# First norm of a decoder trunk: squares of two token chunks summed with tokens on the partitions, channel factors put into x

## The chip, the cores and the metric

The kernel runs on one core of a Trainium2 chip. The metric is the device time of one execution in microseconds. The engines are PE (matmul), PEld (its weight loads), DVE (VectorE), ACT (ScalarE), POOL (GpSimd) and SP (the queue that issues most DMAs).

## The reference, cut to what matters

A trunk of two layers works on 1040 tokens (16 meta tokens and 1024 inputs) of 1024 channels: a Conformer convolution layer, then a differential-attention layer, then a last norm. Only the start of the first layer matters here:

```
def rms_norm(x, gain):
    y = x * lax.rsqrt(jnp.mean(x * x, axis=-1, keepdims=True) + EPS)
    return y * gain

proj = jnp.einsum("bld,dc->blc", rms_norm(h, norm_gain[0]), w_in)
u, g, z = jnp.split(proj, 3, axis=-1)          # 2048 channels each
v = u * jax.nn.sigmoid(g)
v = depthwise convolution over 31 tokens of v  # then a layer norm, silu, times silu(z), a projection
```

So each token has one scale, the inverse root of the mean of its squared channels, and each channel one factor, `norm_gain`.

## The kernel before, in words

Everything is kept with channels on the partitions: `x_t[k]` (k = 0 to 7) holds 128 channels by 1040 tokens in float32, the tokens ordered even ones first, then odd ones. A projection is made as three passes of matmuls with operands split in a high part (rounded to the matmul's float32r) and a low part (the rest): high by high, high by low, low by high (`passes`, L202 to L209). A weight strip is 1024 channels by 128 outputs: it is loaded into `wf` (L174), copied to `wh` by ACT (L190), and `wl` is the difference (L191, written by the helper `lo_part`, L158). `wh` and `wl` have two buffers each, and so has `wf`. The tokens are taken in three chunks of 348, 346 and 346 (`CH`, L34).

The start of the kernel (L330 to L416) has parts that are called in the order of the string `ORDER` (L70), each for one chunk:

- `unscaled` (u, L379): ACT copies x to the high part (L384), DVE or POOL makes the low part (L386, the string `LOU` says which engine).
- `statistics` (t, L353): the eight tiles are squared, all on ACT for chunks 1 and 2, on ACT and DVE in turn for chunk 0 (L362, L365). Eight matmuls with a matrix of ones (L368, plain float32) sum the squares over all channels and spread the sum over the 128 partitions. `rstd_from` (L211) makes the inverse root on 128 x 346 elements: logarithm, exponential, two more ACT operations (L218 to L225) and two DVE operations (L226, L227), into `n0_r`.
- `first_strips` (p, L399): the strips g and u of the convolution's first channel tile, on the unscaled operands, 24 matmuls each for one chunk.
- `scaled` (s, L388): DVE multiplies x in place by the channel factor and by the token scale (L393), ACT copies the high part (L396), DVE and POOL in turn make the low part (L397). All later strips use these operands.

So the first two strips work on x without its scales. The token scale is put on their results (L473, L478). The channel factor is put on their weights: `prepare` (L167) multiplies the two first `wf` by the factors `mod[:, :, 0]`, one half on DVE and one on POOL (L178, the constant `GE` says which).

The convolution follows (L458 to L535): for each of 16 channel tiles PE makes the strips g and u, ACT and DVE make the gated tile `vr` (two buffers), and the taps are shared by DVE (L525, accumulators `ev` and `od` in PSUM), ACT (L511, products) and POOL (L512, sums of these products, L516 at the end). DVE puts the parts together (L527 to L529). z strips are placed between and behind the tiles. The first tile's gate, L473 to L486, uses the token scales; its tanh waits, by `issue_after(last_exp)`, for the exponential of chunk 2's norm, so that the table of functions is changed once.

The Tile framework puts the instructions of each engine in order by a simulation of the timeline, in which an instruction has the rank of its place in the program; `high_priority(offset=n)` ranks those inside n places earlier. The gate of the first tile has 500 (`HP`, L466), the inverse root 2000 (`SP_R`, L376). On the chip every engine and every DMA queue then keeps that order. SP loads, in order: the channel factors of the model, the first strip, chunk 0 of x (half of it from ACT's queue), the second strip, chunks 1 and 2 of x (16 loads), the third strip, the convolution's factors `chn`.

Of the kernel before, what the change touches and what calls it, by code (L numbers as in the profile page):

```python
# [19 lines left out]
P = 128  # L20
D = 1024
# [33 lines left out]
NPART = 7  # L55
WARM = 8
WARM_P = 0
SQE = "AVAVAVAV_AAAAAAAA_AAAAAAAA"
SUE = "PPPPPPPP_PPPPPPPP_PPPPPPPP"
LOV = [(0, 2, 4, 6)] * 3  # L60
SOE = "V"
SOH = 0
AGATE = [(7, 0)] * 3 + [(7, 1)] * 4
AQ = "GGGGGGG"
DIR1 = True
LOU = "VGVVVGVV_VVVVVVVG_VVVVVVVG"
GE = ("GV", "VG")
WL = "GG"
SP_R = 2000
ORDER = "u0_t0_p0_u1_t1_p1_t2_s0_u2_p2_s1_s2"  # L70
FC = [(512, 256), (768, 256)]
HXM = 6
WB = 2
# [23 lines left out]
def trunk(  # L97
    ctx: ExitStack,
    tc: tile.TileContext,
    xt: bass.AP,  # L100
    xn: bass.AP,
    conv_in: bass.AP,
    conv_out: bass.AP,
# [53 lines left out]
    def lo_part(eng, out_, full, hi):  # L157
        return eng.tensor_tensor(out=out_, in0=full, in1=hi, op=ALU.subtract)  # L158

    class Weights:  # L160
# [6 lines left out]
        def prepare(self):  # L167
            if self.done == len(self.order):
                return
            n = self.done  # L170
            src, eng = self.order[n]
            self.done += 1
            wf = gp.tile([P, KD, P], F32, tag="wf", name=f"wf{n}", bufs=2)
            SP.dma_start(out=wf, in_=src)  # L174
            if n < 2:
                for q in range(2):
                    ks = slice(4 * q, 4 * q + 4)
                    (V if GE[n][q] == "V" else G).tensor_tensor(  # L178
                        out=wf[:, ks], in0=wf[:, ks], in1=mod[:, ks, 0:1].to_broadcast([P, 4, P]), op=ALU.mult
                    )  # L180
            keep = self.kept.get(n - len(self.order))
            if keep:
                wh, wl = keep()
            elif n in self.staged:
                wh, wl = stage(0, f"wh{n}", F32R), scratch[-1].tile([P, T], F32R, tag="vr", name=f"wl{n}", bufs=VR)
                wh, wl = [t[:, :D].rearrange("p (k c) -> p k c", c=P) for t in (wh, wl)]
            else:
                wh = gp.tile([P, KD, P], F32R, tag="wh", name=f"wh{n}", bufs=WB)
                wl = gp.tile([P, KD, P], F32R, tag="wl", name=f"wl{n}", bufs=WB)
            A.activation(out=wh, in_=wf, func=AF.Copy)  # L190
            lo_part(eng, wl, wf, wh.bitcast(F32))  # L191
            self.ready.append((wh, wl))
# [113 lines left out]
    with ExitStack() as st0:  # L306
# [4 lines left out]
        def big(name, dt=F32):  # L311
            return sb.tile([P, T], dt, tag="big", name=name, bufs=16)
# [4 lines left out]
        def pair(name):  # L317
            return ps.tile([P, 1024], F32, tag="eo", name=name, bufs=2)
# [21 lines left out]
        n0_r = buf("row", "n0_r")  # L340
        A.preload_act_table_set("natural_log_exp_and_others")
        last_exp = None
        sq_t = [big(f"sq{k}") for k in range(KD)]
        x_sum = pair("n0")
        last_pair = pair("gu0")

        def load(ci):
            c0, w = CH[ci]
# [4 lines left out]
        def statistics(ci):  # L353

            c0, w = CH[ci]
            cs = slice(c0, c0 + w)
            acc = x_sum[:, 512 * (ci % 2) : 512 * (ci % 2) + w]
            tot, started = {}, False
            for k in range(KD):
                sq = sq_t[k][:, cs]  # L360
                if SQE.split("_")[ci][k] == "A":
                    A.activation(out=sq, in_=x_t[k][:, cs], func=AF.Square)  # L362
                else:
                    e = V if SQE.split("_")[ci][k] == "V" else G
                    e.tensor_tensor(out=sq, in0=x_t[k][:, cs], in1=x_t[k][:, cs], op=ALU.mult)  # L365
                e = SUE.split("_")[ci][k]
                if e == "P":
                    PE.matmul(acc, ones, sq, start=not started, stop=k == KD - 1 and not tot)  # L368
                    started = True
                else:  # L370
                    if e in tot:
                        (V if e == "V" else G).tensor_tensor(out=sq, in0=sq, in1=tot[e], op=ALU.add)
                    tot[e] = sq
            for n, sq in enumerate(tot.values()):
                PE.matmul(acc, ones, sq, start=not started and n == 0, stop=n == len(tot) - 1)
            with tc.high_priority(offset=SP_R):  # L376
                return rstd_from(acc, n0_r, 1.0 / D, c0, w, None, True, True)

        def unscaled(ci):  # L379

            c0, w = CH[ci]
            cs = slice(c0, c0 + w)
            for k in range(KD):
                A.activation(out=hh[k][:, cs], in_=x_t[k][:, cs], func=AF.Copy)  # L384
                e = V if LOU.split("_")[ci][k] == "V" else G
                lo_part(e, hl[k][:, cs], x_t[k][:, cs], hh[k][:, cs].bitcast(F32))  # L386

        def scaled(ci):  # L388
            c0, w = CH[ci]
            cs = slice(c0, c0 + w)  # L390
            for k in range(KD):
                t = x_t[k][:, cs]
                V.scalar_tensor_tensor(  # L393
                    out=t, in0=t, scalar=mod[:, k, 0:1], in1=n0_r[:, cs], op0=ALU.mult, op1=ALU.mult
                )
                A.activation(out=hh[k][:, cs], in_=t, func=AF.Copy)  # L396
                lo_part(V if k in LOV[ci] else G, hl[k][:, cs], t, hh[k][:, cs].bitcast(F32))  # L397

        def first_strips(ci):  # L399
            for n, (kind, w_) in enumerate((("g", gw), ("u", uw))):  # L400
# [8 lines left out]
        load(1)  # L409
        load(2)  # L410
        gw, uw = weights.get(), weights.get()
        parts = {"u": unscaled, "p": first_strips, "t": statistics, "s": scaled}
        for step in ORDER.split("_"):
            e = parts[step[0]](int(step[1]))
            if step == "t2":
# [818 lines left out]
def _arrays(i):  # L1234
    h = np.concatenate([i["meta_tokens"], i["x"][0]], axis=0)
    chan = np.concatenate(
        [i["conv_dw_kernel"][0], i["conv_dw_bias"], i["conv_ln_gain"], i["conv_ln_bias"]], axis=0
    )
    model = np.stack([i["norm_gain"][0], i["norm_gain"][1], i["final_norm_gain"]])
    c = np.arange(T, dtype=np.float32)[None, :]  # L1240
    d = np.arange(P, dtype=np.float32)[:, None] + np.float32(912) - c
    return {
        "xt": np.concatenate([h[0::2], h[1::2]], axis=0).T.reshape(KD, P, T),
        "xn": h.T.reshape(KD, P, T),
        "conv_in": _strips(i["conv_w_in"][0]),
        "conv_out": _strips(i["conv_w_out"][0]),
        "attn_in": _strips(i["attn_w_in"][0]),
        "attn_out": _strips(i["attn_w_out"][0]),
        "chan": chan.reshape(TAPS + 3, CT, P).transpose(2, 1, 0),
        "model": model.reshape(3, KD, P).transpose(2, 1, 0),  # L1250
        "lam_vec": np.stack(
            [i["attn_lambda_q1"][0], i["attn_lambda_k1"][0], i["attn_lambda_q2"][0], i["attn_lambda_k2"][0]]
        )[None],
        "subln": i["attn_subln_gain"][0][:, None],
        "dist": np.where(d >= 0, d, np.float32(BIG)).astype(np.float32),
    }
# [22 lines left out]
```

## Time and profile before

| | us |
|---|---|
| median of 3 runs | 1468.19 (1466.68 to 1470.46) |
| profiled execution | 1470.63 |
| its span | 1468.9 |
| PE busy | 1425.6 |
| DVE busy | 1113.2 |
| ACT busy | 887.0 |
| POOL busy | 817.6 |

The span runs from the first to the last instruction that the profile shows. Busy time is the union of an engine's instructions. In rows of groups, the columns are: line, engine, operation, output and inputs with their shapes, count, then busy time in us and mean duration of one in ns, then the idle time of the engine just before them with what ended it. In rows of the timeline: start, length of the merged stretch, engine, line, operation, count, and in brackets the idle time before and what ended it. Records of neighbouring instructions overlap, so the distance of two starts is often less than one duration. A plain float32 matmul leaves two records.

### The profile page before, as it was taken

The numbers are of one execution on the slowest core, as the hardware profiler recorded it, in microseconds if no ns is written. First come the engines' busy times: TensorE is split into PE (matmuls) and PEld (weight loads), VectorE is DVE, ScalarE is ACT, GpSimd is POOL, SyncE is SP. The second block draws the span as 40 slices with busy tenths as digits, with TensorE's granted clock in tenths as the row PEclk, the third lists the DMA queues.
The fourth block names the chain that finished last, engine by engine and source line by source line (L and its number), as shares of the span: only waits on it lengthen the run. The fifth ranks groups of instructions, "written<-read, shape, count | busy, mean of one in ns | idle before, by whom it ended". The sixth has DMA issues, their size and how long they took to land.

```text
span 1468.9 us, 24139 instructions
## 1 busy us (share of the span) xinstructions
PE 1425.6 (97%) x8828; PEld 1335.9 (91%) x8828; DVE 1113.2 (76%) x2100; ACT 887.0 (60%) x1615; POOL 817.6 (56%) x653
## 2 busy tenths in 40 slices
PE   8999999999999999999999999999999999998987
PEld 7999999999999999899998878988889899896877
DVE  7989899899899988978545311577788787786773
ACT  7565655565555658766224311668778777786651
POOL 4598999999999940044014501625345354263572
PEclk9999999999999999999999999999999999999998
DMA  5021111112111332654544634223222322337632
GB/s 182 29 73 44 58 56 61 44 44 73 58 44 44 111 107 88 196 160 152 172 154 138 194 107 113 76 70 96 80 81 67 108 86 71 113 101 253 190 141 74
DMA packets 79929, 150.83 MB, mean 103 GB/s; under 512 B 6977, under 2 KB 46402, under 8 KB 78786
## 3 DMA queue, kind: packets, MB, share of 16 engines
q1 hardware_dynamic: 64802, 123.01, 26.4%
q0 software_dynamic: 5728, 17.04, 3.7%
q10 hardware_dynamic: 9280, 9.23, 2.0%
q8 instruction: 69, 1.13, 0.3%
q14 instruction: 50, 0.41, 0.1%
HBM read 106.73 MB, written 34.01 MB: 96 GB/s over the span
## 4 chain that ended last, share of the span: by engine, by line
PE 50%; POOL 17%; DVE 13%; ACT 8%; issue 8%; DMA 4%; SPq 0%; POOLq 0%; DVEq 0%; ACTq 0%
POOL pb L512 16%; PE c L208 8%; PE v L208 6%; PE q L208 5%; PE k L208 5%; PE za L208 5%; PE ao L208 4%; PE o L208 3%; ACT pr L511 2%; PE u L208 2%; PE z L208 2%; DVE wl L158 2%; PE s L990 2%; PE s L991 2%; PE tp L1024 2%
## 5 line engine op out<-in xcount | busy, mean ns | idle before, releaser
L512 POOL TENSOR_TENSOR pb<-pr,pb 128x521 f32<-128x521 f32 (+1 forms) x272 | 389.2, 1440 | 24.9 <-ACT pr L511 10.4
L511 ACT ACTIVATE pr<-vr,chn 128x521 f32<-128x521 f32 x224 | 150.6, 725 | 122.8 <-POOL pb L512 122.3
L208 PE MATMUL c<-b,wh 128*128 128x260 f32 x1024 | 188.3, 286 | 3.1 <-DVE b L158 1.7
L525 DVE SCALAR_TENSOR_TENSOR ev<-vr,chn,ev 128x520 f32<-128x520 f32 x240 | 181.2, 755 | 1.2
L190 ACT ACTIVATE wh<-wf 128x1024 fp32r<-128x1024 f32 x115 | 120.9, 1052 | 97.8 <-PE c L208 54.0
L208 PEld LDWEIGHTS c<-b,wh 128*128 128x128 f32 x1024 | 160.8, 192 | 3.8 <-DVE b L158 1.9
L208 PE MATMUL g<-hp,wh 128*128 128x346 f32 (+1 forms) x752 | 151.8, 329 | 7.3 <-ACT hp L384 3.4
L208 PE MATMUL u<-hp,wh 128*128 128x346 f32 (+1 forms) x752 | 155.9, 321 | 2.1 <-ACT wh L190 2.1
L208 PE MATMUL c<-b,wl 128*128 128x260 f32 x512 | 146.0, 287 | 2.5 <-DVE wl L158 2.4
L158 DVE TENSOR_TENSOR wl<-wf,wh 128x1024 fp32r<-128x1024 f32 x81 | 118.9, 1469 | 29.7 <-ACT wh L190 29.0
L208 PE MATMUL z<-hp,wh 128*128 128x346 f32 (+1 forms) x768 | 135.6, 321 | 0.5 <-ACT sig L470 0.5
L208 PEld LDWEIGHTS g<-hp,wh 128*128 128x128 f32 x752 | 127.4, 193 | 9.3 <-ACT hp L384 3.7
L158 POOL TENSOR_TENSOR wl<-wf,wh 128x1024 fp32r<-128x1024 f32 x34 | 84.9, 2499 | 90.9 <-ACT wh L190 39.2
L525 DVE SCALAR_TENSOR_TENSOR od<-xs,wc,od 128x520 f32<-128x520 f32 x176 | 132.6, 754 | 0.0
L697 POOL TENSOR_TENSOR total<-hsq,total 128x520 f32<-128x520 f32 x12 | 20.6, 1715 | 196.1 <-DMA xr<-xn 99.2
L208 PEld LDWEIGHTS u<-hp,wh 128*128 128x128 f32 x752 | 125.7, 188 | 3.0 <-ACT wh L190 3.0
L208 PEld LDWEIGHTS z<-hp,wh 128*128 128x128 f32 x768 | 124.3, 188 | 0.9 <-ACT sig L470 0.7
L998 ACT ACTIVATE p<-p,st 128x272 f32<-128x272 f32 (+7 forms) x128 | 100.5, 785 | 36.1 <-DVE st L993 35.5
L208 PEld LDWEIGHTS c<-b,wl 128*128 128x128 f32 x512 | 98.4, 192 | 3.2 <-DVE wl L158 3.0
L208 PE MATMUL g<-hp,wl 128*128 128x346 f32 (+1 forms) x376 | 84.2, 322 | 0.0
L208 PE MATMUL v<-wv,g 128*128 128x512 f32 x352 | 83.5, 394 | 0.0
L990 PE MATMUL s<-k,q 128*128 128x256 f32 (+6 forms) x224 | 76.8, 347 | 3.5 <-DVE st L993 3.5
(292 smaller groups left out, 3473.1 us busy)
## 6 DMA issues: line engine op xcount, KB each, us to landing
wf<-conv_in SPq DMA_DIRECT2D x48, 512.0 KB, 3.5
wf<-conv_out SPq DMA_DIRECT2D x32, 512.0 KB, 4.2
wf<-attn_in SPq DMA_DIRECT2D x32, 512.0 KB, 3.7
wf<-attn_out SPq DMA_DIRECT2D x17, 512.0 KB, 3.8
sz_d<-sz ACTq DMA_DIRECT2D x32, 260.0 KB, 4.4
szr<-sz_d SPq DMA_DIRECT2D x16, 520.0 KB, 4.4
v<-v_d POOLq DMA_DIRECT2D x8, 1024.0 KB, 5.4
ya_d<-yb SPq DMA_DIRECT2D x28, 256.0 KB, 2.5
```

The lines of the kernel that those rows point to most:

```text
L158: return eng.tensor_tensor(out=out_, in0=full, in1=hi, op=ALU.subtract)
L190: A.activation(out=wh, in_=wf, func=AF.Copy)
L208: PE.matmul(o, a[k], b[k], start=start and i == 0, stop=stop and i == tot - 1)
L511: A.activation(out=d, in_=src, func=AF.Copy, scale=w)
L512: G.tensor_tensor(out=dst, in0=d, in1=dst, op=ALU.add)
L525: V.scalar_tensor_tensor(out=dst, in0=src, scalar=w, in1=dst, op0=ALU.mult, op1=ALU.add)
L697: (V if SQA[m] == "V" else G).tensor_tensor(out=total[:, ns], in0=sq, in1=total[:, ns], op=ALU.add)
L990: PE.matmul(o[:, :wm], q2[m][:, qs], k2[m][:, c0 : c0 + wm], start=True, stop=False)
L991: PE.matmul(o[:, :wm], q2[m][:, qs], kl2[m][:, c0 : c0 + wm], start=False, stop=True)
L998: A.activation(out=p[:, :n], in_=p[:, :n], func=AF.Exp, scale=-1.0, bias=least, accum_out=st[:, 1:2],)
L1024: PE.transpose(tp[:, (kb - kb0) * P : (kb - kb0 + 1) * P], p0[:, kb * P : (kb + 1) * P], ident)
```

## The change

Chunk 0's statistics stay as they are (its squares lie in other buffers). For chunks 1 and 2 the tokens are loaded a second time with tokens on the partitions: a new input `xk` holds the last 692 tokens as rows of 1024 channels, and `load_tokens` (k) loads six blocks of 115 or 116 rows. One operation squares a block and sums it along the row (`accum_out`): two blocks of a chunk on ACT, one on DVE. The inverse root is then made on columns of three numbers. To spread it over the partitions, DVE multiplies the identity by the column, which gives a diagonal, and one matmul of ones by the diagonal writes the scale of 115 tokens on all partitions, in PSUM. The scaling of x reads it there; ACT copies it to `n0_r` for the first tile's gate. The channel factors go from the two first weight strips into the unscaled operands: the ACT copy takes them as its scale, and the low part, now always on DVE, becomes one operation of x, factor and high part. The order of the parts changes.

```
-ORDER = "u0_t0_p0_u1_t1_p1_t2_s0_u2_p2_s1_s2"
+ORDER = "u0_t0_p0_u1_p1_u2_k0_s0_t1_p2_t2_s1_s2"
-SQE = "AVAVAVAV_AAAAAAAA_AAAAAAAA"
+SQE = "AVAVAVAV"
+TKE = "AVA_AVA"
...
             SP.dma_start(out=wf, in_=src)
-            if n < 2:
-                for q in range(2):
-                    ks = slice(4 * q, 4 * q + 4)
-                    (V if GE[n][q] == "V" else G).tensor_tensor(
-                        out=wf[:, ks], in0=wf[:, ks], in1=mod[:, ks, 0:1].to_broadcast([P, 4, P]), op=ALU.mult
-                    )
...
+        TB = [(c0 - CH[1][0] + o, n) for c0, w in CH[1:] for o, n in ((0, 116), (116, 115), (231, 115))]
+        x_k = [big(f"xk{b}")[:, :D] for b in range(6)]
+        tk = sb.tile([P, 4, 6], F32, name="tk")
+        V.memset(tk, 1.0)
...
+            bs = slice(3 * ci - 3, 3 * ci)
+            for b in range(6)[bs]:
+                r0, n = TB[b]
+                t = x_k[b][:n]
+                if TKE.split("_")[ci - 1][b % 3] == "A":
+                    A.activation(out=t, in_=t, func=AF.Square, accum_out=tk[:n, 0, b : b + 1])
                 else:
+                    V.tensor_tensor_reduce(
+                        out=t, in0=t, in1=t, scale=1.0, scalar=0.0, op0=ALU.mult, op1=ALU.add,
+                        accum_out=tk[:n, 0, b : b + 1],
+                    )
             with tc.high_priority(offset=SP_R):
-                return rstd_from(acc, n0_r, 1.0 / D, c0, w, None, True, True)
+                s, x, t, r = (tk[:, j, bs] for j in range(4))
+                V.tensor_scalar(out=x, in0=s, scalar1=1.0 / D, scalar2=EPS, op0=ALU.mult, op1=ALU.add)
+                e = row_rstd(x, r, t)
+                for b in range(6)[bs]:
+
+                    r0, n = TB[b]
+                    o = r0 + CH[1][0] - c0
+                    dg = small(f"dg{b}", w=n)
+                    V.tensor_scalar(out=dg[:n], in0=ident[:n, :n], scalar1=tk[:n, 3, b : b + 1], scalar2=None, op0=ALU.mult)
+                    PE.matmul(acc[:, o : o + n], ones[:n], dg[:n], start=True, stop=True)
+                scale_of[ci] = acc
+                A.activation(out=n0_r[:, cs], in_=acc, func=AF.Copy)
+            return e
...
             for k in range(KD):
-                A.activation(out=hh[k][:, cs], in_=x_t[k][:, cs], func=AF.Copy)
-                e = V if LOU.split("_")[ci][k] == "V" else G
-                lo_part(e, hl[k][:, cs], x_t[k][:, cs], hh[k][:, cs].bitcast(F32))
+                g0 = mod[:, k, 0:1]
+                A.activation(out=hh[k][:, cs], in_=x_t[k][:, cs], func=AF.Copy, scale=g0)
+                V.scalar_tensor_tensor(
+                    out=hl[k][:, cs], in0=x_t[k][:, cs], scalar=g0, in1=hh[k][:, cs].bitcast(F32),
+                    op0=ALU.mult, op1=ALU.subtract,
+                )
...
                 V.scalar_tensor_tensor(
-                    out=t, in0=t, scalar=mod[:, k, 0:1], in1=n0_r[:, cs], op0=ALU.mult, op1=ALU.mult
+                    out=t, in0=t, scalar=mod[:, k, 0:1], in1=scale_of[ci], op0=ALU.mult, op1=ALU.mult
                 )
...
+        def load_tokens(_):
+            for (r0, n), t in zip(TB, x_k):
+                SP.dma_start(out=t[:n], in_=xk[r0 : r0 + n])
...
+        "xk": h2[CH[1][0] :],
```

## Rows read from the trace of the kernel before

**Rows 1.** The page, part 1: busy time, share of the span and instructions.

```profile
PE 1425.6 (97%) x8828; PEld 1335.9 (91%) x8828; DVE 1113.2 (76%) x2100; ACT 887.0 (60%) x1615; POOL 817.6 (56%) x653
```

**Rows 2.** Windows: stretch, length, busy time (count) by engine, granted clock, DMA.

```profile
8.50:23.30 14.80, 14.79 (x64) 12.05 (x65) 14.68 (x19) 13.77 (x35) 10.26 (x6) 1.00 0.89 305
23.30:48.00 24.70, 24.69 (x130) 21.17 (x128) 22.01 (x36) 17.00 (x39) 10.00 (x9) 1.00 0.01 3
48.00:66.00 18.00, 16.27 (x93) 16.27 (x94) 18.00 (x32) 9.63 (x19) 6.25 (x5) 0.91 0.17 59
```

**Rows 3.** The convolution: one window, and a wait (us in total, times, longest).

```profile
240.00:260.00 20.00, 20.00 (x128) 20.00 (x127) 20.00 (x31) 11.31 (x17) 19.21 (x13) 1.00 0.17 54
...
DVE v L528 <- POOL pb L516: 26.3, 11, 4.2
```

**Rows 4.** The chain that ended last, behind the convolution.

```profile
534.80 29.05 PE z L208 x183
```

**Rows 5.** The timeline of PE from 0 to 66 us.

```profile
1.37 3.78 PE L339 MATMUL warm<-ident,ones 128*128 128x128 f32 x16 [1.37 <-POOL ident masks.py:199]
8.51 1.43 PE L208 MATMUL g<-hp,wh 128*128 128x348 f32 x3 [3.36 <-ACT hp L384]
...
26.21 4.82 PE L368 MATMUL n<-sq,ones 128*128 128x346 f32 x16
30.60 1.37 PE L208 MATMUL g<-hp,wl 128*128 128x346 f32 x6
...
49.73 4.67 PE L208 MATMUL g<-hp,wh 128*128 128x348 f32 x18 [1.75 <-ACT wh L190]
```

**Rows 6.** The timeline of all engines, from 5 to 8 us.

```profile
5.43 1.55 POOL L178 TENSOR_TENSOR wf<-wf,mod 128x512 f32<-128x512 f32 x1 [4.12 <-DMA wf<-conv_in]
6.00 2.23 DVE L365 TENSOR_TENSOR sq<-x 128x348 f32<-128x348 f32 x3
...
7.01 1.06 ACT L190 ACTIVATE wh<-wf 128x1024 fp32r<-128x1024 f32 x1 [4.98 <-POOL wf L178]
```

**Rows 7.** Groups of DVE's instructions from 0 to 66 us, shapes apart.

```profile
L158 DVE TENSOR_TENSOR hp<-x,hp 128x346 fp32r<-128x346 f32 x22 | 15.1, 736 | 2.1 <-ACT hp L384 2.0
L393 DVE SCALAR_TENSOR_TENSOR x<-x,mod,n_r 128x346 f32<-128x346 f32 x16 | 10.8, 742 | 0.0
...
L178 DVE TENSOR_TENSOR wf<-wf,mod 128x512 f32<-128x512 f32 x2 | 1.4, 685 | 4.3 <-DMA wf<-conv_in 4.3
...
L227 DVE SCALAR_TENSOR_TENSOR n_r<-rs_x,n_r 128x346 f32<-128x346 f32 x2 | 1.0, 513 | 0.0
...
L486 DVE TENSOR_TENSOR vr<-gu,sig 128x346 f32<-128x346 f32 x1 | 0.5, 503 | 0.0
```

**Rows 8.** Groups of the whole span that resemble the added operations.

```profile
L993 DVE CUSTOM_DVE_ANT_0 p<-s,total 128x456 f32<-128x456 f32 x16 | 10.0, 622 | 0.2
...
L993 DVE CUSTOM_DVE_ANT_0 p<-s,total 128x264 f32<-128x264 f32 x16 | 6.8, 427 | 5.0 <-PE tp L1024 4.1 <-PE s L991 0.7
...
L809 DVE TENSOR_SCALAR sub_s<-sub_g 128x1 f32<-128x1 f32 x1 | 0.1, 140 | 0.0
...
L998 ACT ACTIVATE p<-p,st 128x1040 f32<-128x1040 f32 x16 | 18.6, 1163 | 12.9 <-DVE st L993 12.9
```

**Rows 9.** Two lines of DVE in the convolution: duration ns min/median/max, first and last start.

```profile
L488 DVE TENSOR_TENSOR xs<-vr x16: 703/955/1789, 64.5 to 482.9; 128x535 f32<-128x535 f32 x16
...
L482 DVE SCALAR_TENSOR_TENSOR vr<-sig,u x60: 318/409/517, 65.1 to 481.2; 128x348 f32<-128x348 f32 x15, 128x172 f32<-128x172 f32 x15, 128x174 f32<-128x174 f32 x15, 128x346 f32<-128x346 f32 x15
```

**Rows 10.** SP's issues of chunks 1 and 2, and their size and time to landing.

```profile
6.82 8.31 SPq L351 DMA_DIRECT2D x<-xt  x16
...
x<-xt SPq DMA_DIRECT2D x16, 173.0 KB, 4.2
```

**Rows 11.** The timeline of DVE: chunk 2's scale, the first tile's last product.

```profile
49.76 0.51 DVE L227 SCALAR_TENSOR_TENSOR n_r<-rs_x,n_r 128x346 f32<-128x346 f32 x1
...
63.41 0.50 DVE L486 TENSOR_TENSOR vr<-gu,sig 128x346 f32<-128x346 f32 x1
```

More of the change, by code (lines that the diff above doesn't have):

```diff
@@ L57 @@
 WARM_P = 0
-SQE = "AVAVAVAV_AAAAAAAA_AAAAAAAA"
-SUE = "PPPPPPPP_PPPPPPPP_PPPPPPPP"
+SQE = "AVAVAVAV"
+TKE = "AVA_AVA"
 LOV = [(0, 2, 4, 6)] * 3
@@ L65 @@
 DIR1 = True
-LOU = "VGVVVGVV_VVVVVVVG_VVVVVVVG"
-GE = ("GV", "VG")
 WL = "GG"
 SP_R = 2000
-ORDER = "u0_t0_p0_u1_t1_p1_t2_s0_u2_p2_s1_s2"
+ORDER = "u0_t0_p0_u1_p1_u2_k0_s0_t1_p2_t2_s1_s2"
 FC = [(512, 256), (768, 256)]
@@ L100, in trunk @@
     xt: bass.AP,
+    xk: bass.AP,
     xn: bass.AP,
@@ L342, in trunk @@
         last_exp = None
-        sq_t = [big(f"sq{k}") for k in range(KD)]
+        sq_t = [t[:, n : n + CH[0][1]] for t in (big("sq0"), big("sq2"), hsum, stage(0, "sq6")) for n in (0, CH[0][1])]
+        TB = [(c0 - CH[1][0] + o, n) for c0, w in CH[1:] for o, n in ((0, 116), (116, 115), (231, 115))]
+        x_k = [big(f"xk{b}")[:, :D] for b in range(6)]
+        tk = sb.tile([P, 4, 6], F32, name="tk")
+        V.memset(tk, 1.0)
         x_sum = pair("n0")
         last_pair = pair("gu0")
+        scale_of = {}
         def load(ci):
@@ L357, in statistics @@
             acc = x_sum[:, 512 * (ci % 2) : 512 * (ci % 2) + w]
[L358 to L362, printed above, removed]
-                else:
[L364 to L373, printed above, removed]
@@ L374, in statistics @@
-            for n, sq in enumerate(tot.values()):
-                PE.matmul(acc, ones, sq, start=not started and n == 0, stop=n == len(tot) - 1)
-            with tc.high_priority(offset=SP_R):
-                return rstd_from(acc, n0_r, 1.0 / D, c0, w, None, True, True)
+            if ci == 0:
+                for k in range(KD):
+                    sq = sq_t[k]
+                    if SQE[k] == "A":
+                        A.activation(out=sq, in_=x_t[k][:, cs], func=AF.Square)
+                    else:
+                        V.tensor_tensor(out=sq, in0=x_t[k][:, cs], in1=x_t[k][:, cs], op=ALU.mult)
+                    PE.matmul(acc, ones, sq, start=k == 0, stop=k == KD - 1)
+                scale_of[ci] = n0_r[:, cs]
+                with tc.high_priority(offset=SP_R):
+                    return rstd_from(acc, n0_r, 1.0 / D, c0, w, None, True, True)
@@ L411, in trunk @@
         gw, uw = weights.get(), weights.get()
-        parts = {"u": unscaled, "p": first_strips, "t": statistics, "s": scaled}
+        parts = {"u": unscaled, "p": first_strips, "t": statistics, "s": scaled, "k": load_tokens}
         for step in ORDER.split("_"):
@@ L1241, in _arrays @@
     d = np.arange(P, dtype=np.float32)[:, None] + np.float32(912) - c
+    h2 = np.concatenate([h[0::2], h[1::2]], axis=0)
     return {
-        "xt": np.concatenate([h[0::2], h[1::2]], axis=0).T.reshape(KD, P, T),
+        "xt": h2.T.reshape(KD, P, T),
+        "xk": h2[CH[1][0] :],
         "xn": h.T.reshape(KD, P, T),
```

## The prediction

> **What bounds the kernel now.** I read the engines' totals first: the matmul engine is busy for 97% of the span [rows 1], so work taken from PE is worth time wherever PE has no slack. The change lies in the first 66 us, so I then cut that stretch at the first matmul of the projections (8.5), at the end of chunk 0's strips (23.3) and at the end of chunk 2's (48.0) [rows 2]. PE has no listed idle time from 8.5 to 48, and DVE is as full: 14.68 of 14.80 us, then 22.01 of 24.70, then 18.00 of 18.00. ACT and POOL have room. So two engines set the pace of the start, and a gain has to come out of both, or the later one must have somewhere to catch up.
>
> What follows the start decides how much of a gain is kept. In a typical 20 us of the convolution PE is full (128 records, 0.156 us each) and POOL is at 19.21, while DVE waits 26.3 us in 11 places for POOL's last subtraction of a tile [rows 3]. So the convolution is paced by POOL and PE together; DVE can catch up there by 2 to 4 us a tile. When the convolution ends, the chain runs through 29.05 us of PE's z strips [rows 4]. The end therefore comes earlier by about the smaller of two numbers: how much earlier PE gets through its strips, and how much earlier POOL can begin its first tile.
>
> **PE, step by step.**
> - Removed: the sums of squares of chunks 1 and 2. One takes 16 records and holds PE from 26.21 to the next strip's matmul at 30.60, 4.4 us [rows 5]; there are two, 8.8 us.
> - Added: six matmuls of the diagonals, about 115 columns each. Plain float32 makes two records of a matmul, so 12. By columns, a record of 346 costs 4.39/16 = 0.27 us, and one of 115 a third of it: 1.1 us in all. The warm-up at the start is nearer in size: 16 records of 128 columns in 3.78 us, 0.24 each [rows 5], 2.8 us in all. I take 2.8, with 1.1 as the other end. Net 6.0, at most 7.7.
> - The start: the first wh waited 4.98 us, until POOL's scaling of wf, which began at 5.43 and took 1.55, and PE's first matmul came at 8.51, after ACT's first copy of x; x itself was there at 6.00 [rows 5, 6]. Without the scaling ACT can begin as soon as wf has landed, 1.5 us earlier. Between 8.5 and 23.3 PE's work is 48 records of 0.156 and 16 of 0.27, 11.9 of 14.8 us, so 2.9 us of that stretch are short waits for operands. The lead of 1.5 may be lost in them (0), or they may shrink too, since ACT and DVE lose work there (4.4). I take 1.5.
> [...]
>
> PE's sum: 6.0 + 1.5 = 7.5 us.
>
> **DVE, step by step.** Removed: two scalings of half a weight strip, 0.69 each, and four norm operations of chunks 1 and 2, 0.51 each [rows 7]: 3.4 us. Added: four low parts that POOL made, 0.51 each, 2.0. Two reductions over 1024 elements: the nearest rows are 622 ns for 456 elements and 427 for 264, about 1.0 ns an element, so 1.2 each [rows 8], 2.4. For each chunk four operations on three columns at 0.14 [rows 8], and three diagonals of 115 columns between 0.14 and the 0.51 of 346 columns; at 0.25 that is 1.3, 2.6 for both. Together 7.0, net 3.6 us more.
>
> Against this stands what the operations share with POOL. The scaling of x for chunks 1 and 2 has a mean of 742 ns with both operands in SBUF; the multiply whose one operand is in PSUM takes 503 at the same size [rows 7]. Over the whole convolution, where POOL hardly rests, the add of two SBUF tiles spreads from 703 to 1789 ns, and the multiply with a PSUM operand never exceeds 517 [rows 9]. The change hands those 16 scalings their factor in PSUM: 16 x 0.235 = 3.8 us less (0 if they stay as they are). POOL also drops two scalings and four low parts, some 7 us of work beside which DVE's low parts ran at 736 instead of 507 ns, up to 31% lost, 2.2 us; I take half, 1.1. And DVE's 2.0 us of waiting for ACT's copies [rows 7] should go, because ACT no longer squares two chunks in between (0 if it doesn't). Sum: 3.6 - 3.8 - 1.1 - 2.0 = 3.3 us less, between 3.6 more and 4.4 less.
>
> [...]
>
> **Loads and the order.** SP gains six loads behind those of x: 2.83 MB, as much as chunks 1 and 2 of x, whose 16 issues took 8.31 us up to 15.1, each landing 4.2 us later [rows 10]. So the last token rows land at about 15.1 + 0.4 + 8.3 + 4.2 = 28 us. The channel factors, next on that queue, move back by the same 8.3 us, and only the taps need them. Squaring a block on ACT costs about 1.2 us (the 1040-element row) [rows 8], and the small chain behind it (four operations of 0.14, two on ACT, three diagonals, their matmuls, a copy) some 3 more, so chunk 2's scale exists at about 33, where it now ends at 50.3 [rows 11]. That scale is now what the first tile's last gate waits for; from there DVE needs another 13 us, full of other work, before the tile's last product at 63.41 [rows 11]. With the scale early, that product waits for chunk 2's strips on PE (48.0 - 7.5 = 40.5), and for its turn on DVE. The code ranks these gate operations 500 instructions ahead of the scalings of chunks 1 and 2, so I expect them before most of those, and POOL's start earlier by more than 7.5 us. Even if DVE's total shrinks by only 3.3, what it puts off is made up while it would wait for POOL [rows 3]. DMA has nothing else to do from 24 to 50, so the added bytes hide.
>
> **The forecast.** PE's 7.5 us is the smaller number, and the end moves by it. The profiled execution took 1470.63 us, 1.7 around its span of 1468.9, and lies 2.4 over the median of 1468.19; the sum is a difference, so I set it against the median: 1468.2 - 7.5 = 1460.7. Its own bounds, 0 to 4.4 for the start and 1.1 to 2.8 for the diagonals, give 1456 to 1463.7. What a measurement here can tell from no change is about 0.3%, 4.4 us.
>
> **Rivals.**
> - *DVE's order keeps the first tile late.* If the gate operations still come after all scalings, POOL starts earlier only by DVE's 3.3 us, and POOL paces the convolution: 1464.9, between 1461 and 1469. For it: DVE has no idle time from 48 to 66 [rows 2]. Against: the rank, and the scale 17 us earlier. Chance 0.17.
> - *The gap goes too.* If ACT has wh ready when the second tile's strips begin, 1.75 + 1.9 us come on top, and a little of the short waits: 1468.2 - 7.5 - 3.6 - 1 = 1456. For it: ACT loses squares and half its norm work. Against: the buffer is freed no sooner before it is needed. Chance 0.13.
> - *Slower: DVE stands at the head of its queue for token rows.* DVE runs in order. If its two reductions are placed before the scalings of chunk 0, at about 16, it waits for the second block (15.5 + 2.8 + 4.2 = 22.5) and again for the fifth (26.6): up to 6.5 + 4 = 10.5 us, in a stretch without slack. The strips of the second tile then lack scaled operands and PE idles. The price is 10.5 - 3.3 = 7 us: 1475. It decides once these waits exceed some 8 us; at 3 they only take DVE's gain. For it: the loads are last in the queue. Against: the order puts the reductions after chunk 0's scalings, which can't start before its strips are read, near 20. Chance 0.10.
>
> The forecast keeps 0.60. That the change doesn't remove what it says is excluded by its loops: 16 squares and 16 sums have no other place.
>
> **How the numbers follow.** Faster by over 0.3%: the forecast, the second rival, and the small part of the first under 1463.8, 0.74. Within 0.3%: the rest of the first, and slight waits for the loads, 0.15. Slower: 0.11. From 1454 to 1467 lie the forecast, most of the first rival and half or more of the second, a little over 8 in 10.
>
> **What would show it.** Right: PE's records of the squares' sums down from 48 to 16 with 12 short ones added; chunk 2's strips ended near 40; first matmul near 7; scalings of chunks 1 and 2 near 510 ns beside POOL; POOL's first add before 57; the z strips at the convolution's end beginning some 7.5 us before 534.8 [rows 4]. Wrong: DVE or ACT idle before a token-row operation; PE idle between 35 and 60 with a lower granted clock; POOL's first add after 60; or an early start lost again to waits of POOL or PE before those strips.

## The result and the profile after

The changed kernel takes 1480.34 us (median of 6 runs, 1476.09 to 1482.53) against 1468.86 for the kernel before in the same comparison (6 runs, 1466.37 to 1470.46): a ratio of 1.0075, 95% interval 1.006 to 1.0089. It is **slower by 11 us**, where 7.5 us less were forecast; the range ended at 1467. The profiled execution took 1481.2 us, its span is 1479.4.

The page's first part, as [rows 1]: PE and POOL have lost 7 us of work each, DVE and ACT hardly anything. So the engines' totals don't hold the loss; it must be waiting.

```profile
PE 1418.6 (96%) x8808; PEld 1329.7 (90%) x8808; DVE 1111.4 (75%) x2117; ACT 885.9 (60%) x1605; POOL 810.2 (55%) x647
```

The windows of [rows 2], of the kernel after (stretch, length, busy time and count of PE, PEld, DVE, ACT, POOL, granted clock, DMA share, GB/s):

```profile
8.50:23.30 14.80, 14.80 (x65) 12.04 (x65) 14.80 (x26) 13.22 (x28) 2.92 (x2) 1.00 0.88 301
23.30:48.00 24.70, 14.83 (x95) 14.55 (x93) 9.49 (x19) 6.30 (x14) 2.67 (x3) 0.85 0.31 118
48.00:66.00 18.00, 12.35 (x58) 12.07 (x59) 16.23 (x42) 12.48 (x28) 4.18 (x4) 0.63 0.20 59
```

The middle window is the one to look at. All five engines do less in it: PE has 14.83 of 24.70 us where it had 24.69, DVE 9.49 where it had 22.01. What moves is the DMA, and slowly: 118 GB/s, where the stretch before it has 301.

PE's timeline from 0 to 66 us, as [rows 5] (start, duration, what, in brackets the idle time before it and what ended it):

```profile
7.11 1.61 PE L201 MATMUL g<-hp,wh 128*128 128x348 f32 x3 [1.96 <-ACT hp L400]
...
36.70 1.43 PE L201 MATMUL gu<-hp,wl 128*128 128x346 f32 x8
53.10 1.63 PE L389 MATMUL n<-dg,ones 116*128 116x116 f32 x6 [14.98 <-DVE dg L388]
55.28 1.63 PE L389 MATMUL n<-dg,ones 116*128 116x116 f32 x6 [0.55 <-ACT n_r L391]
56.59 4.89 PE L201 MATMUL g<-hp,wh 128*128 128x348 f32 x16
```

The first matmul comes 1.4 us earlier and chunk 2's strips end 10 us earlier, at 38.1. Then PE stands for 14.98 us until DVE has the first diagonals, and it comes back slower: the next strip's 16 records take 4.89 us at a granted clock of 0.50, the u strip after it 2.71 at 1.00, as these windows show.

```profile
56.70:61.20 4.50, 4.50 (x18) 4.50 (x17) 4.10 (x9) 2.79 (x6) 0.93 (x1) 0.50 0.21 82
62.90:65.50 2.60, 2.60 (x19) 2.60 (x18) 2.60 (x6) 2.60 (x8) 1.80 (x2) 1.00 0.00 0
```

Why the diagonals are late stands in the timeline of all engines, at the operations that read the token rows:

```profile
16.76 12.61 SPq L419 DMA_DIRECT2D xk<-xk  x5
...
26.21 1.06 ACT L373 ACTIVATE xk<-xk 116x1024 f32<-116x1024 f32 x1 [4.49 <-DMA xk<-xk]
...
27.27 0.48 ACT L218 ACTIVATE rs_t<-n_r 128x348 f32<-128x348 f32 x1
...
31.40 1.23 DVE L375 CUSTOM_DVE_ANT_0 xk<-xk 115x1024 f32<-115x1024 f32 x1 [3.10 <-DMA xk<-xk]
...
33.10 4.02 DVE L411 SCALAR_TENSOR_TENSOR x<-x,mod,n_r 128x348 f32<-128x348 f32 x8
...
35.22 1.06 ACT L373 ACTIVATE xk<-xk 115x1024 f32<-115x1024 f32 x1 [7.47 <-DMA xk<-xk]
...
40.30 1.06 ACT L373 ACTIVATE xk<-xk 116x1024 f32<-116x1024 f32 x1 [3.54 <-DMA xk<-xk]
...
43.83 1.83 DVE L375 CUSTOM_DVE_ANT_0 xk<-xk 115x1024 f32<-115x1024 f32 x1 [6.20 <-DMA xk<-xk]
...
47.84 1.06 ACT L373 ACTIVATE xk<-xk 115x1024 f32<-115x1024 f32 x1 [4.47 <-DMA xk<-xk]
```

The six blocks become usable at 26.2, 31.4, 35.2, 40.3, 43.8 and 47.8: one each 4.3 us ((47.84 - 26.21) / 5), some 470 KB at about 110 GB/s. The second to the sixth come 5.2, 3.8, 5.1, 3.5 and 4.0 us after the one before; the first and the fourth have 116 rows, the others 115. Both engines stand there with ready work behind. ACT stands at the first block with chunk 0's own scale behind it: L218 starts at 27.27, though its input (L212) was written from 21.24 on in 0.48 us. DVE stands at the second: chunk 0's L220, whose input (L219) was written from 27.79 on in 0.52 us, comes after it at 32.55, and the scalings of chunk 0 (L411) at 33.10. The channel factors, next on SP's queue, hold DVE to 48.33.

The waits from 0 to 66 us (in total, times, longest), and the DMA view from 0 to 60 (40 slices of 1.5 us):

```profile
ACT xk L373 <- DMA xk<-xk: 20.0, 4, 7.5
...
PE n L389 <- DVE dg L388: 15.0, 1, 15.0
...
DVE xk L375 <- DMA xk<-xk: 9.3, 2, 6.2
```

```profile
GB/s 0 211 322 359 386 265 314 332 373 371 354 357 322 270 107 112 128 126 120 128 131 131 229 123 125 100 109 104 104 106 83 42 0 0 0 85 265 177 172 0
```

At 21 us the rate falls from 270 to between 100 and 131 GB/s and stays there until 45, but for one slice: the stretch of the token rows and, behind them, the factors.

POOL's first add comes 9 us later than in the kernel before (the first of these lines is of before, the second of after), and the z strips behind the convolution 8.4 us after the 534.80 of [rows 4]:

```profile
65.37 26.43 POOL L512 TENSOR_TENSOR pb<-pr,pb 128x521 f32<-128x521 f32 x18 [5.14 <-ACT pr L511]
```

```profile
74.40 26.85 POOL L534 TENSOR_TENSOR pb<-pr,pb 128x521 f32<-128x521 f32 x18 [2.27 <-ACT pr L533]
```

```profile
543.19 28.92 PE z L201 x183
```

So the loss arises in the first 75 us and is carried to the end.

### The profile page after: what moved, and what is told of

Read it like the earlier page. It is cut to its first block, busy times and chain, and to the rows that moved or that the text cites. A ratio compares the mean times of both kernels' runs of the same rounds, so it can differ in the third digit from the quotient of the medians.

```text
span 1479.4 us, 24093 instructions
## 1 busy us (share of the span) xinstructions
PE 1418.6 (96%) x8808; PEld 1329.7 (90%) x8808; DVE 1111.4 (75%) x2117; ACT 885.9 (60%) x1605; POOL 810.2 (55%) x647
## 4 chain that ended last, share of the span: by engine, by line
PE 51%; POOL 19%; DVE 11%; issue 7%; DMA 6%; ACT 5%; SPq 1%; POOLq 0%; DVEq 0%; ACTq 0%
POOL pb L534 17%; PE c L201 9%; PE v L201 6%; PE k L201 6%; PE q L201 5%; PE za L201 5%; PE ao L201 4%; PE z L201 4%; PE o L201 3%; PE s L1012 2%; PE s L1013 2%; PE tp L1046 2%; ACT pr L533 2%; DVE wl L157 2%; DMA a<-ya_d 1%
## 5 line engine op out<-in xcount | busy, mean ns | idle before, releaser
L201 PE MATMUL u<-hp,wh 128*128 128x346 f32 (+1 forms) x752 | 150.3, 321 | 4.8 <-ACT wh L183 3.3
L201 PE MATMUL g<-hp,wh 128*128 128x346 f32 (+1 forms) x752 | 147.4, 327 | 3.0 <-ACT hp L400 2.0
L157 DVE TENSOR_TENSOR wl<-wf,wh 128x1024 fp32r<-128x1024 f32 x81 | 118.8, 1468 | 33.6 <-ACT wh L183 32.7
L201 PE MATMUL g<-hp,wl 128*128 128x346 f32 (+1 forms) x376 | 80.5, 321 | 0.0
```

What stands on the lines that cost most here:

```text
L201: PE.matmul(o, a[k], b[k], start=start and i == 0, stop=stop and i == tot - 1)
```

## The experiments

Three theories of the late rows were to be told apart. **A**: a load of 116 or 115 rows is carried by few of the DMA engines, so the way the rows are cut sets its time. **B**: the order is at fault: in-order engines stand for these rows, however they are cut. **C**: 2.8 MB more is too much in itself.

For A speaks the DMA share of the changed kernel: 1.02 at 346 GB/s from 16 to 20 us, while the loads of x still land, but 0.32 at 126 from 24 to 32 and 0.25 at 103 from 38 to 46, five and four of the 16 engines.

**1 and 2. The rows cut otherwise.** Once into blocks of 128, 128 and 90 rows, and once with each load in two parts, 112 rows and the rest:

```diff
-... for o, n in ((0, 116), (116, 115), (231, 115))]
+... for o, n in ((0, 128), (128, 128), (256, 90))]
```

```diff
-                SP.dma_start(out=t[:n], in_=xk[r0 : r0 + n])
+                SP.dma_start(out=t[:112], in_=xk[r0 : r0 + 112])
+                SP.dma_start(out=t[112:n], in_=xk[r0 + 112 : r0 + n])
```

> Same kernel as the changed one, but the token rows of a chunk are cut in blocks of 128, 128 and 90 instead of 116, 115 and 115. Theory A (a load of 115 or 116 rows is spread over few DMA engines, and the late token rows are the whole loss): the six loads run near 340 GB/s instead of some 115, the last one lands before 31 us instead of 47.8, PE's wait of 15 us for the diagonals is gone, and the time falls under that of the kernel before: about 1461 us, 1455 to 1466. Theory B (it is the order: in-order waits of ACT and DVE for a second copy of x, however it is cut): the rows still come late to their queues, time 1472 to 1480. Theory C (the 2.8 MB themselves are too much): no change, 1478 to 1482.

> Same kernel as the changed one, with its blocks of 116 and 115 tokens, but each load is issued as two: 112 rows, then the last 4 or 3. Theory A: the same as with blocks of 128, within 4 us of that run, since only the way the loads spread over the DMA engines differs from the changed kernel; the last rows land before 32 us. Theory C: 1478 to 1482. If blocks of 128 help and this does not, it is the shape of the squares and diagonals and not the loads.

Measured: 1469.9 us with 128 rows (ratio 1.0005, 0.9996 to 1.0015) and 1468.06 in two parts (0.9995, 0.9985 to 1.0004). The whole loss of 11 us is gone with the same bytes, from the same queue and called at the same place in the program; A's 1455 to 1466 us were missed all the same. With 128 rows, the timeline of all engines has the last block at 33.42, 14 us earlier, and PE's wait is down to 3.16:

```profile
33.42 1.06 ACT L373 ACTIVATE xk<-xk 90x1024 f32<-90x1024 f32 x1 [0.70 <-DMA xk<-xk]
...
40.33 0.90 PE L389 MATMUL n<-dg,ones 128*128 128x128 f32 x6 [3.16 <-DVE dg L388]
41.78 1.69 PE L389 MATMUL n<-dg,ones 128*128 128x128 f32 x6 [0.55 <-ACT n_r L391]
...
43.19 3.76 PE L201 MATMUL g<-hp,wh 128*128 128x348 f32 x16
...
47.33 3.96 DVE L411 SCALAR_TENSOR_TENSOR x<-x,mod,n 128x346 f32<-128x346 f32 x8
```

B and C fall as causes of the loss. For B it is the run with 128 rows that shows it: ACT has the same order as in the change, and on DVE the first reduction still stands ahead of chunk 0's scalings (26.39 against 27.55; only chunk 0's scale, L220, now comes before it), but both engines together stand 6.3 us for these rows where they stood 29.3. With loads in two parts the framework made another order (the scalings at 24.68, the reduction at 29.31), so that run alone would not part A from B. But neither version is faster than the kernel before, although PE starts the second tile's strips 6.5 and 8.1 us earlier (43.19 and 41.65 against 49.73 [rows 5]). That is a second question.

**3. The cut made worse.** Blocks of 113, 113 and 120 rows:

```diff
+... for o, n in ((0, 113), (113, 113), (226, 120))]
```

> Same kernel as the changed one, blocks of 113, 113 and 120 tokens. [...] If loads are only slower when the rows are not a multiple of 16, whatever their divisors: as the changed kernel within 5 us. Theory B or C: as the changed kernel.

Measured, in a single run: 1531.29 us, 51 more than the change, and the last block is used at 95.97 (30 to 50 us and 88 were the author's estimate, from four such loads one after the other, each at a quarter of the change's 107 GB/s, 17 us). The rows, in the timeline; then the window of 56 to 76 us and PE's wait:

```profile
37.45 1.06 ACT L373 ACTIVATE xk<-xk 113x1024 f32<-113x1024 f32 x1 [15.25 <-DMA xk<-xk]
...
57.28 1.23 DVE L375 CUSTOM_DVE_ANT_0 xk<-xk 113x1024 f32<-113x1024 f32 x1 [17.75 <-DMA xk<-xk]
58.41 1.06 ACT L373 ACTIVATE xk<-xk 120x1024 f32<-120x1024 f32 x1 [19.43 <-DMA xk<-xk]
```

```profile
56.00:76.00 20.00, 0.00 (x0) 0.00 (x0) 6.19 (x13) 1.64 (x3) 0.00 (x0) 0.50 0.07 26
```

```profile
PE n L389 <- DVE dg L388: 63.4, 1, 63.4
```

A block of 113 rows takes 20 us (37.45 to 57.28), the block of 120 behind it 1 us more. While one of 113 is under way alone, the DMA share is 0.07, one engine of 16 (0.0625), at 26 GB/s; in the change it was 0.32 at 126 and then 0.25 at 103 (above). Five times 26 GB/s are 130 and four times 104, near the two levels of the change's slices: mostly 120 to 131 up to 37.5 us, 100 to 109 from there to 45. So a block of 113 rows moves as one engine would, and the change's blocks of 116 and 115 together as five would, then as four; which of the two sizes gives which number is not shown. PE stands for 63.4 us. A holds from both sides.

**4 and 5. The two halves of the change apart.** First the channel factors in x, with the statistics as before; then the statistics alone (loads in two parts), with the factors on the weights as before:

```diff
-                A.activation(out=hh[k][:, cs], in_=x_t[k][:, cs], func=AF.Copy)
-                e = V if LOU.split("_")[ci][k] == "V" else G
-                lo_part(e, hl[k][:, cs], x_t[k][:, cs], hh[k][:, cs].bitcast(F32))
+                A.activation(out=hh[k][:, cs], in_=x_t[k][:, cs], func=AF.Copy, scale=g0)
+                V.scalar_tensor_tensor(out=hl[k][:, cs], in0=x_t[k][:, cs], scalar=g0, in1=hh[k][:, cs].bitcast(F32), ...)
```

> The kernel before with one part of the change alone: the channel factors go into x (ACT's copy takes them as scale, all low parts on DVE), the weights are no longer scaled; the statistics stay as they were. The prediction's step gives PE's first matmul near 7.0 instead of 8.5 and, if the lead is kept, 1.5 us less: 1466 to 1468. Rival: the lead is lost in the short waits of the first strips or DVE's four added low parts cost it, 1468.5 to 1471.

> The other part of the change alone, with well-cut loads: squares of the two chunks with tokens on the partitions and scales spread by a diagonal, but the channel factors on the two first weight strips and the low parts divided between DVE and POOL as before. The factors alone made no difference. If the two parts simply add, this is as the kernel with both, 1467 to 1469. If DVE is what both press on (theory F), the statistics alone are faster than both, since four low parts stay on POOL: 1465 to 1467; if the factors' earlier start is needed to keep PE ahead, slower: 1469 to 1472.

Measured: the factors alone 1469.38 us (1.0006, 0.9997 to 1.0016), nothing, as the rival has it. PE's first matmul comes at 7.62 and the second tile's strips begin at 47.77, 2.0 us earlier, but from 56 to 60 us PE waits 1.09 for ACT and 1.75 for DVE, and POOL's first add, at 65.14, is where it was. The statistics alone take 1467.36 (0.9981, 0.9972 to 0.9991), 2.8 us less. The second half is worth a little, and the first adds nothing to it that these runs show; it hands DVE the four low parts that POOL made before. Whether it takes something away, as theory F (DVE is full, see 6 to 8) has it, is not shown: 1467.36 lies in the range of the plain sum, and the intervals of the two versions overlap.

**6 to 8. Earlier rows, and squares off DVE.** Theory **D**: the scales are still late and hold PE. Theory **F**: DVE is full, and its turn for the first tile is what is late. One version has chunk 1's rows loaded ahead of chunk 2 of x, one all squares on ACT, one both:

```diff
         load(1)
+        load_tokens(range(3))
         load(2)
+        load_tokens(range(3, 6))
```

```diff
-TKE = "AVA_AVA"
+TKE = "AAA_AAA"
```

> The kernel with the loads cut in 112 rows and the rest, and its token rows loaded earlier: chunk 1's before chunk 2 of x, chunk 2's right behind it. Theory D (what is left of the forecast's gain is lost because the scales still come late: PE stands some 3 us for the diagonals near 37 and runs at the lower clock behind it): chunk 1's rows land before 23 us, PE's wait for the diagonals falls under 1 us, and the time is 3 to 5 us less than with late rows: 1463 to 1465. Theory F (DVE, which has no idle time from 24 to 66, holds the first tile back whatever the rows do): within 1.5 us of the kernel with late rows, 1467 to 1469. Chunk 2 of x comes later by 4 us, which should hurt nothing, as its strips begin near 29.

> The kernel with the loads cut in 112 rows and the rest, with all six blocks squared on ACT, none on DVE. It takes 2 x 1.3 us from DVE. Theory F: POOL's first add comes about 2.5 us earlier (57 instead of 59.9) and the time falls by 2 to 3 us, to 1465 to 1466. Theory D: ACT squares three blocks one after the other, so the scales come no earlier, and the time stays within 1.5 us of 1468.

> Token rows earlier and all squares on ACT together. If theories D and F each hold a part, this is the fastest, 1461 to 1464; if D alone, as the run with earlier rows; if F alone, as the run with the squares on ACT; if neither, near 1468.

Measured: 1476.14 (1.0043, 1.0031 to 1.0055), 1469.1 (0.9994, 0.9984 to 1.0003) and 1476.09 (1.0042, 1.0029 to 1.0054). Earlier rows made it worse, by about 7 us against the late ones (1.0043 against 0.9995): a miss, and D with it in this form. The rows did come earlier, but so did the work on them. Two of chunk 0's squares on DVE come at 20.73 and 21.94, behind the first reduction, and ACT's chains of chunks 1 and 2, and the table load for the gates behind them, stand ahead of chunk 0's logarithm. In the timeline of all engines chunk 0's sums, two table loads and its scale stand at

```profile
26.65 2.50 PE L364 MATMUL n<-sq,ones 128*128 128x348 f32 x8
...
33.84 1.28 ACT L211 ACT_TABLE_LOAD   x1
...
36.15 1.28 ACT L212 ACT_TABLE_LOAD   x1
...
39.05 0.52 DVE L220 SCALAR_TENSOR_TENSOR n_r<-rs_x,n_r 128x348 f32<-128x348 f32 x1
```

where the version with 128 rows has that scale (L220) at 24.98. Chunk 0's scalings and the first gate wait for it. Squares on ACT take the two reductions from DVE, 2.5 us, but put the diagonals behind ACT (PE waits 3.57 and 2.09 us there), and POOL's first add comes at 63.04 instead of 59.90, where F had 57; D's range, within 1.5 us of 1468, is met. So neither tells F from its rivals.

**9. Meant as the upper bound.** The sums of chunks 1 and 2 left out altogether; chunk 0's scale is used in their place:

```diff
-            bs = slice(3 * ci - 3, 3 * ci)
...
+            scale_of[ci] = n0_r[:, CH[0][0] : CH[0][0] + w]
+            e = A.activation(out=n0_r[:, cs], in_=scale_of[ci], func=AF.Copy).ins
```

> Leaves out part of the computation: the sums of squares of chunks 1 and 2 with their diagonals and the token rows; their scale is taken from chunk 0's. It is the most that any way of getting these sums could give at the start: PE has no sums and no diagonals, DVE no reductions, SP no extra loads. Theory K (what the start gains is kept): PE begins the second tile's strips near 39, POOL's first add comes near 55 and the convolution ends near 521, 10 us before the kernel before; the time follows by about as much, 1458 to 1460. Theory G (what the start gains is given back behind the convolution, whatever made it): POOL's first add and the convolution's end come as early as that, but of the 10 us no more than 3 reach the end, 1465 to 1469; the stages from the variance sums to the softmax eat the rest.

Measured: 1466.61 us (0.9983, 0.9973 to 0.9992), 2.85 less than before. PE begins the second tile's strips at 39.46 and POOL adds from 60.84 only; the timelines of PE, DVE and POOL:

```profile
39.46 1.91 PE L201 MATMUL g<-hp,wh 128*128 128x348 f32 x9 [2.07 <-ACT wh L183]
```

```profile
58.88 0.50 DVE L485 TENSOR_TENSOR vr<-gu,sig 128x346 f32<-128x346 f32 x1
```

```profile
60.84 26.51 POOL L511 TENSOR_TENSOR pb<-pr,pb 128x521 f32<-128x521 f32 x18 [4.29 <-ACT pr L510]
```

PE's lead of 10.3 us is one of 4.5 at DVE's last product of the tile (63.41 in [rows 11]) and at POOL (65.37). K's step to POOL near 55 fails, and the end is in G's range.

But this run is not the bound that it was meant to be. The edit also takes the scale of chunks 1 and 2 out of PSUM, and their 16 scalings become slower. DVE's groups from 0 to 66 us, with loads in two parts and in this run:

```profile
L411 DVE SCALAR_TENSOR_TENSOR x<-x,mod,n 128x346 f32<-128x346 f32 x16 | 8.3, 564 | 0.0
```

```profile
L389 DVE SCALAR_TENSOR_TENSOR x<-x,mod,n_r 128x346 f32<-128x346 f32 x16 | 13.9, 910 | 0.0
```

These 5.6 us are about what the reductions, the small operations and the diagonals had cost DVE (6.1 us with loads in two parts). So DVE was not made free, and POOL's first add is 0.9 us later than the 59.90 with the sums in place. Left out in this way the sums are worth 2.85 us; **what the best way of getting them could give is not shown**.

**10. The best of the above with 128 rows.** The statistics alone, with the blocks of 1:

> The statistics alone (channel factors on the weights as before), with blocks of 128, 128 and 90 rows, each in one load. Theory F (DVE's time decides, the way of loading the same bytes does not once all engines share them): as the statistics alone with loads in two parts, 1466 to 1468.5, 0 to 3 us before the kernel before. If the cut of the loads still matters, 1469 to 1471.

Measured: 1466.86 us (0.9981, 0.9972 to 0.9989), as the statistics alone with loads in two parts. Between these two cuts it makes no difference. This version beats both kernels, the one before by 2.6 us.

**11. Less on DVE.** The change with loads in two parts, and eight low parts less (left out; the strips there use those of the unscaled x):

```diff
-                lo_part(V if k in LOV[ci] else G, hl[k][:, cs], t, ...)
+                if ci == 0 or k not in LOV[ci]:
+                    lo_part(V if k in LOV[ci] else G, hl[k][:, cs], t, ...)
```

> The change with loads in two parts, and eight operations less on DVE: the low parts of chunks 1 and 2 that DVE makes after the scalings (four a chunk, 0.51 to 0.83 us each, some 4 to 6 us) are left out, so that the strips there run on with the low parts of the unscaled x. PE's work is the same. Theory F (DVE holds the first tile back): POOL's first add comes 4 us or more before the 59.90 of the loads in two parts, near 55 to 56, and the convolution ends as much earlier, near 520. If PE or ACT holds it, POOL's first add stays within 1.5 us of 59.90. Behind the convolution, theory G (given back) has the end at 1464 to 1469 all the same, theory K (kept) at 1462 to 1464.

Measured: 1465.64 us (0.997, 0.9959 to 0.9982). POOL's timeline and the window of 48 to 66 us, first with loads in two parts, then with less on DVE:

```profile
59.90 26.81 POOL L535 TENSOR_TENSOR pb<-pr,pb 128x521 f32<-128x521 f32 x18 [2.27 <-ACT pr L534]
```

```profile
48.00:66.00 18.00, 17.23 (x108) 16.69 (x107) 18.00 (x32) 11.14 (x23) 12.51 (x11) 1.00 0.00 0
```

```profile
56.51 26.31 POOL L536 TENSOR_TENSOR pb<-pr,pb 128x521 f32<-128x521 f32 x18 [1.99 <-ACT pr L535]
```

```profile
48.00:66.00 18.00, 18.00 (x116) 18.00 (x115) 17.30 (x29) 14.46 (x27) 15.54 (x14) 1.00 0.04 6
```

PE starts the second tile's strips at the same time (41.73 and 41.65), DVE is no longer full, the tile's last product on DVE comes at 53.81 instead of 57.92, and POOL begins 3.4 us earlier; 4 or more were expected. F holds for the first tile: its strips are done at 38.2, and DVE holds it back, not PE. It fits run 9 too, where DVE was full. The convolution's end did not follow by as much: the sums of the means come 1.5 us earlier (524.4 and 522.9). The time is in G's range.

**Where the rest is given back.** Five points of the traces side by side, in us:

| kernel | POOL's first add | sums of the means | sums of the variance | span | time against before |
|---|---|---|---|---|---|
| before | 65.37 | 531.0 | 563.7 | 1468.9 | |
| after | 74.40 | 539.4 | 572.0 | 1479.4 | 1.0075 |
| loads in two parts | 59.90 | 524.4 | 558.6 | 1466.3 | 0.9995 |
| statistics alone, 128 rows | 62.55 | 527.0 | 559.5 | 1463.5 | 0.9981 |
| no statistics | 60.84 | 525.1 | 559.3 | 1464.8 | 0.9983 |
| less on DVE | 56.51 | 522.9 | 555.3 | 1465.9 | 0.997 |

A lead at POOL passes through the convolution nearly whole (5.5 becomes 6.6, 8.9 becomes 8.1). Behind it two losses can be read. The first: PE's timeline at the sums of the means with loads in two parts, and windows over these sums with loads in two parts, in the kernel before, and with less on DVE.

```profile
524.42 1.86 PE L571 MATMUL mean_ps<-hsum,ones 128*128 128x260 f32 x4 [1.84 <-DVE v L551]
```

```profile
524.50:528.30 3.80, 3.80 (x10) 3.03 (x11) 1.79 (x2) 0.00 (x0) 0.00 (x0) 0.55 1.01 262
```

```profile
531.10:534.40 3.30, 3.30 (x15) 2.88 (x16) 1.80 (x2) 0.00 (x0) 0.00 (x0) 1.00 0.98 277
```

```profile
522.90:526.10 3.20, 3.20 (x16) 2.79 (x16) 0.45 (x1) 0.00 (x0) 0.00 (x0) 1.00 0.87 250
```

With loads in two parts PE, now ahead, stands 1.84 us for the last tile's `v`, and 10 of these 16 records run in a window with a granted clock of 0.55: all take 5.46 us in place of 3.77, so the lead of 6.6 is 5.1 at the variance. The length of the stand alone doesn't decide this. With the statistics alone and 128 rows PE stands 2.12 us at the same place and goes on at a granted clock of 1.00:

```profile
527.02 1.15 PE L575 MATMUL mean_ps<-hsum,ones 128*128 128x260 f32 x4 [2.12 <-DVE v L555]
```

```profile
527.00:530.30 3.30, 3.28 (x15) 2.88 (x16) 1.89 (x2) 0.00 (x0) 0.00 (x0) 1.00 0.96 273
```

With less on DVE PE doesn't stand there, and 8.4 of lead are left at the variance, of which 3.8 reach the time. The second loss is one of this version, in the attention of the second layer, where PE needs a load (`kl`). PE's timeline before and with less on DVE:

```profile
1324.47 0.39 PE L991 MATMUL s<-kl,q 128*128 128x256 f32 x1 [0.95 <-DMA kl<-kl]
...
1326.16 0.39 PE L991 MATMUL s<-kl,q 128*128 128x256 f32 x1 [0.74 <-DMA kl<-kl]
```

```profile
1320.86 0.58 PE L1015 MATMUL s<-kl,q 128*128 128x256 f32 x1 [3.14 <-DMA kl<-kl]
```

PE comes to it 5.8 us earlier than before (1317.20 and 1323.01 for the last `za` strip), but the load is there only 3.6 earlier; PE stands 3.14 us, goes on at a granted clock of 0.81 in the window of 1318 to 1327, and 2.8 of lead are left at the next strips (`ao`, 1324.58 and 1327.41). With loads in two parts the lead falls there only from 2.66 to 2.25. The other steps between the variance and the end are smaller, some of them gains, and their causes stay open. The profiled executions of before and of less on DVE lie 2.4 and 2.1 over their medians, so some 2 us of a difference in spans are scatter.

## Why the prediction was wrong

**The step that failed** is the one on the loads: "So the last token rows land at about 15.1 + 0.4 + 8.3 + 4.2 = 28 us." It took the rate of the loads of x, full tiles of 128 rows [rows 10], for loads of 116 and 115. The last rows landed at 47.8, 20 us later. With it fell "DMA has nothing else to do from 24 to 50, so the added bytes hide": they fill that time at a third of the rate. With 128 rows in a load the last block was used at 33.42, still 5 us behind the 28.

**The rival that came** is the slower one. DVE did stand at the head of its queue, before chunk 0's scalings (31.40, ahead of 33.10), for 9.3 us in two places; 6.5 and 4 were its price. But ACT's 20.0 us, with chunk 0's scale behind the first block, and the strip at a granted clock of 0.50 were not in it, and in place of its price of 7 us the runs show 11.5. What was held against it (the reductions come after the scalings) was an assumption about the order that no row showed.

**PE's sum** came out once the loads are well cut: 7.5 us forecast, 6.5 and 8.1 measured at the start of the second tile. Several terms hold: first matmul at 7.11 in the change (forecast 7.0), 12 records of diagonals in 2.6 us with 128 rows (0.90 + 1.69; forecast 2.8), 3.3 in the change at a granted clock of 0.50. Part of the agreement is luck: PE's stands before the diagonals (3.16 + 0.55 us with 128 rows, 1.19 + 0.55 in two parts) were not in the sum, and the gap of 1.75 us before the second tile [rows 5], for which the sum has no term, is gone, as the second rival had it. The rival's other 1.9 us are the 4.67 of the 18 records behind the gap, at a granted clock of 0.62 in the kernel before, less 2.8 at 0.156 each; part of them stays, as 16 records there take 3.76 us with 128 rows and 3.59 in two parts, where the u strip behind them takes 2.70. The forecast's own bounds are added up wrongly: 0 to 4.4 for the start and 1.1 to 2.8 for the diagonals give 1456 to 1462.2, not 1463.7; the measured time is far outside either.

**DVE's terms** were near: the 16 scalings with a PSUM operand have a mean of 564 ns (run 9's first line), where 742 were and 507 were forecast, so 2.8 of the 3.8 us came; the reductions took 1.21 to 1.83 us plus 0.08 for the accumulator (1.2), a diagonal 0.27 (0.25). Eight scalings in a row take 3.96 us with an operand in PSUM (run 1) and 4.02 with both in SBUF (33.10 in the change). But their sum left DVE full from 48 to 66, as in [rows 2].

**The second step that failed** is "The end therefore comes earlier by about the smaller of two numbers", with POOL's start taken as the larger one. POOL was the smaller: first add at 59.90 to 62.55 in the versions with well-cut loads (runs 1, 2, 5 and 10), not before 57, which the first rival named (DVE's order keeps the first tile late) and run 11 shows. And even the smaller one doesn't reach the end: 5.5 us at POOL are 0.9 in the time with loads in two parts (1468.06 against 1468.97), 8.9 are 3.8 in run 11. Part of it goes where PE, ahead, stands for another engine or a load (1.84 and 3.14 us, above). So with the loads mended the forecast would still have been 7 us too low.

**The factors' half** was given PE's 1.5 us at the start. Alone, 0.9 come there (7.62 against 8.51) and 2.0 at the second tile, and nothing is left at POOL or in the time (run 4).

## What to carry to other kernels

Price a load by its own row count, not by the rate of its neighbours: 113 rows took 20 us, 115 or 116 some 4.3, one of 120 was there 1 us after one of 113; loads of 112 rows and the rest cost nothing here. Where an in-order engine reads a late load, list what is queued behind that read on each such engine before calling the bytes hidden. A lead made on one engine is worth what the slowest of its partners keeps of it, and what later loads leave of it. And when work is left out to find a bound, look whether the edit changes the operands of what remains: run 9 slowed 16 scalings from 564 to 910 ns and so bounds nothing.

## What the runs showed that had not been expected

- A load of 113 rows moves at 26 GB/s with a DMA share of 0.07; loads of 115 and 116 rows at 118 with 0.31; the same bytes in blocks of 128 or of 112 and a rest raise no wait for these rows above 4 us.
- A lead can come with a lower clock: with PE ahead, a stand of 1.84 us was followed by 3.8 us at a granted clock of 0.55. But 2.12 us of standing at the same place in run 10, and 1.14 in the kernel before, were followed by 1.00; what decides it is not shown.
